# Projections and six gates of the second block moved into one stage of seven-product pairs

## The chip, the cores and the metric

One core of a Trainium2 chip. The metric is the device time of one execution in microseconds (us), median of the runs. All arrays are float32; one launch computes everything.

## The reference, cut to what matters

Two transformer-like blocks run one after the other on 1024 tokens of width 1024. The change touches only the head of the second one:

```python
xn   = rmsnorm_2(x, attn_norm_g)                  # (1024, 1024)
proj = xn @ w_in                                  # pool 512 | dilated q,k,v 3*768 | stick q,k,v 3*512 | s5 512
y_pool, y_dil, y_sb, y_s5 = pool_mixer(...), dilated_attention(...), stick_breaking_attention(...), s5_mixer(...)
for bi, yb in enumerate((y_pool, y_dil, y_sb, y_s5)):
    gate   = sigmoid(xn @ w_gate[bi])             # 4 gates of 1024 x 1024
    merged = merged + gate * (yb @ w_branch[bi])
x = x + merged @ w_out
```

The four gates depend on `xn` alone; the mixers depend on `proj` alone. Here `x` of the second block is the first block's output after `final_norm`.

## The kernel before, in words

The residual stream lies feature-major: eight tiles of 128 features by 1024 tokens. Every matmul keeps float32 accuracy by three products: an operand is split into a high part (`fp32r`) by ScalarE and the rest by VectorE (`split`, L380 to L387), and `gemm` (L351) adds high*high, high*low and low*high. One **tile** of a projection (128 output features, all 1024 tokens) is 8 steps of the contraction x 3 products x 2 halves of 512 tokens, so 48 matmuls. `load_w` (L326) fetches its 512 KB of weights on SyncE's queue (SP) and splits them.

The feed-forward stages already use another form: `pair` (L886) computes two output tiles together with seven products of half size instead of eight (Strassen-Winograd), each product being 4 steps x 3 = 12 matmuls, so 84 for two tiles. It needs the sums T1 to T4 and quarters B11, B21, B22 of the input (`factors`, L845), four sums of weights on POOL and five adds on VectorE. `up` (L957) starts three pairs side by side and then runs one after the other.

Order of the second block before:

- `block2_norm` (L1566) closes the first block's feed-forward: per half of 512 tokens eight output tiles, two sums of squares (VectorE and POOL), the norm, and the split into `xh`, `xl` (16 slots). `early` runs the left half of two stick projections while the right half's norm is due. The residual goes to DRAM (`xd`).
- `stick` (L1640): v by token-major products, then four heads. Each head runs two `chain`s of latency-bound steps; between them `heads` projects the next head's q and k (2 tiles).
- `dilated` (L1750): three groups. Each projects 4 tiles (q, k), from the second on also 2 tiles of v, then runs 8 softmax steps; its bias table goes through DRAM (`ED`, `hk`).
- `s5` (L1953): a preamble of small VectorE operations beside token-major products, then four quarters `q`. In each quarter POOL builds `CL`, `BL`; PE transposes; VectorE copies `U`, builds `Ec` and `Es`, scans, and forms `Y`. `pool` (L2254) projects 4 tiles on the way. Then the `glu` products.
- `merge` (L2305): loads the gates, multiplies branches, in the order 1, 2, 0, 3.

The 32 gate tiles (`gate`, L2287) are computed as **filler**: `fill` (L300) pops the next gate from a list and is called at set places: 1 in `stick`, 15 in `dilated`, up to 19 in `s5`, of which 16 find a gate. A gate is stored to DRAM and read back by `merge`.

Who orders the work: except in the first stage (`manual_schedule`), a planner at compile time orders each engine's instructions. It prefers program order and lets a later instruction go ahead when the earlier one has no data or no buffer in its model. So buffers decide how far it can reach: big tiles share one set of 31 slots (`s4`), PSUM has two 1024-wide buffers and four of 512, and a stage's own pool of SBUF (`fp`) is free for the next stage's pool only when its tiles are released.

Of the kernel before, what the change touches and what calls it, by code (L numbers as in the profile page):

```python
# [18 lines left out]
P = 128  # L19
D = 1024  # L20
# [17 lines left out]
ORDER = (1, 2, 0, 3)  # L38

# [216 lines left out]
class Kern:  # L256
# [193 lines left out]
    def rstd_twice(self, out1, out2, acc, accg):  # L450
# [11 lines left out]
        self.bcast(out2, r2)  # L462
        self.bcast(out1, r1)

# [492 lines left out]
    def up(self, fp, W, B, steps, hidden):  # L957
# [8 lines left out]
        run = lambda j, *first: self.pair(fp, W[j], W[NF + j], B, lambda a: hidden(j, a), gated, *first)  # L966
        p, q = self.pmm(), self.pmm()
        g = [run(0, (p[:, 0:HT], q[:, HT:T])), run(1, (p[:, HT:T], None)), run(2, (q[:, 0:HT], None))]
        for n in range(6):
            if n > 1:  # L970
                next(steps)
            for i in g:
                next(i)
        next(steps)
        for i in g:
            next(i)
# [3 lines left out]
        for j in range(4, NF):  # L980
# [8 lines left out]
        return out  # L989
# [546 lines left out]
    def block1_ffn(self, xd, B, steps):  # L1536
# [15 lines left out]
        with tc.tile_pool(name="f1d", bufs=1) as fp:  # L1552
# [9 lines left out]
            self.block2_norm(xs, out)  # L1562
# [3 lines left out]
    def block2_norm(self, xs, out):  # L1566
        nc, A = self.nc, self.A
        gg = self.gg
        self.xh = [self.big("xh", F32R) for _ in range(KC)]
        self.xl = [self.big("xl", F32R) for _ in range(KC)]  # L1570
        self.xd = [self.dp.tile([P, T], F32, name=self.nm("xd"), tag=f"xd{k}") for k in range(KC)]
        r1, r2 = self.big("r1"), self.big("r2")

        def norm(k, h):
            sl = slice(h * HT, (h + 1) * HT)
            self.norm_split(xs[k][:, sl], r2[:, sl], gg[:, k : k + 1], None, self.xh[k][:, sl], self.xl[k][:, sl], low=nc.gpsimd if h == 0 else nc.vector)

        self.xh2, self.xl2 = self.halves(self.xh), self.halves(self.xl)
        self.first = []
# [8 lines left out]
        for h in range(2):  # L1588
            sl = slice(h * HT, (h + 1) * HT)
            acc = self.big("acc")  # L1590
            for m in range(KC):
                out(m, h)
                self.sumsq(acc[:, 0:HT], xs[m][:, sl], m == 0)
                self.sumsq(acc[:, HT:T], xs[m][:, sl], m == 0, g=self.smc("final_norm", m), eng=nc.gpsimd)
                if h == 1:
                    norm(m, 0)
            if h == 1:
                early(0)
                early(4)
            self.rstd_twice(r1[:, sl], r2[:, sl], acc[:, 0:HT], acc[:, HT:T])  # L1600
        for k in range(KC):
            norm(k, 1)
        for k in range(KC):
            self.dump(f"x2{k}", xs[k])
            nc.vector.scalar_tensor_tensor(xs[k], xs[k], self.smc("final_norm", k), r1, ALU.mult, ALU.mult)
            nc.sync.dma_start(self.xd[k], xs[k])
            self.dump(f"xb{k}", xs[k])
            if self.dbg and "xn0" in self.dbg:
                self.dump(f"xn{k}", self.xh[k].bitcast(F32))


# [28 lines left out]
    def stick(self):  # L1640
# [4 lines left out]
        def heads(h):  # L1645
            r = []
            for m in (h, 4 + h):
                hi, lo = self.big("sqh", F32R), self.big("sql", F32R)
                scale = 128 ** -0.5 if m < 4 else None
                if h:  # L1650
# [772 lines left out]
```

## Time and profile before

| | us |
|---|---|
| median of 3 runs (3452.68 to 3458.37) | 3456.63 |
| the profiled execution | 3452.84 |
| its span, first to last instruction | 3451.0 |
| TensorE busy, 15699 matmuls | 3312.0 |
| VectorE busy | 2092.2 |
| ScalarE busy | 1311.0 |
| POOL busy | 654.7 |

The page gives busy time per engine, the span in slices, the chain that ended last and the costliest groups; the trace behind it can be asked for a window, a tile or an engine's timeline. Matmuls overlap, so their mean duration (about 400 ns for 512 columns) is longer than the distance from one to the next. In a table of windows the number in brackets is the count of instructions; the last three columns are the granted TensorE clock (1 is full speed), the share of the DMA engines and GB/s.

### The profile page before, as it was taken

What the parts mean: (1) busy time and instruction counts of PE and PEld (TensorE: products, weight loads), DVE (VectorE), ACT (ScalarE), POOL (GpSimd) and SP (SyncE); (2) the same over time, 40 slices, a digit from 0 to 9 for tenths busy, and PEclk for the clock granted to TensorE, in tenths of its full rate; (3) what the DMA queues carried; (4) which work ended last, traced back from release to release, by engine and by line L of the source; (5) the groups of instructions that cost most, each with busy time, mean ns of one, the idle gap of its engine ahead of it and who ended that gap; (6) DMA issues with size and microseconds to landing.
All of it is one profiled execution on the core that took longest, in us unless ns stands there. A gap on an engine that the chain in (4) does not pass through costs nothing. (4 is left out here: it accounts for less than half of the span.)

```text
span 3451.0 us, 42496 instructions
## 1 busy us (share of the span) xinstructions
PE 3312.0 (96%) x15699; PEld 2635.8 (76%) x15699; DVE 2092.2 (61%) x3955; ACT 1311.0 (38%) x2471; POOL 654.7 (19%) x510
## 2 busy tenths in 40 slices
PE   6999998989999999899999999999999989999998
PEld 4797776768888777777877778787878768888777
DVE  8746787686565797677332237466265764434886
ACT  5224655454444334356242332222222443333332
POOL 3200000152221441200000002221032142321530
PEclk9999999999999999999999999999999999999999
DMA  6545112422221432201121112222464322223232
GB/s 235 199 151 181 42 59 90 143 85 81 80 80 58 168 94 84 98 31 37 51 65 52 63 55 97 72 90 87 163 227 156 132 98 86 79 85 126 89 93 78
DMA packets 139953, 348.60 MB, mean 101 GB/s; under 512 B 16713, under 2 KB 41697, under 8 KB 139745
## 3 DMA queue, kind: packets, MB, share of 16 engines
q1 hardware_dynamic: 139744, 345.88, 29.7%
q8 instruction: 124, 2.03, 0.2%
q14 instruction: 85, 0.69, 0.1%
HBM read 270.67 MB, written 75.16 MB: 100 GB/s over the span
## 5 line engine op out<-in xcount | busy, mean ns | idle before, releaser
L382 ACT ACTIVATE wh<-w 128x512 fp32r<-128x512 f32 (+1 forms) x508 | 308.4, 610 | 1035.2 <-PE mm L360 734.5
L383 DVE TENSOR_TENSOR wl<-w,wh 128x512 fp32r<-128x512 f32 (+1 forms) x508 | 365.3, 723 | 512.6 <-ACT wh L382 491.5
L358 PE MATMUL mm<-bh,wh 128*128 128x512 f32 x1376 | 532.9, 401 | 26.7 <-ACT a L904 6.2
L362 PE MATMUL mm<-bh,wl 128*128 128x512 f32 x1376 | 523.6, 396 | 4.0 <-DVE wl L383 3.8
L360 PE MATMUL mm<-bl,wh 128*128 128x512 f32 x1376 | 526.3, 396 | 0.2 <-DVE bl L383 0.2
L358 PEld LDWEIGHTS mm<-bh,wh 128*128 128x128 f32 x1376 | 259.8, 189 | 110.2 <-DVE x L2364 11.7
L362 PEld LDWEIGHTS mm<-bh,wl 128*128 128x128 f32 x1376 | 259.7, 189 | 68.7 <-DVE wl L383 7.6
L362 PE MATMUL mm<-xh,wl 128*128 128x512 f32 x944 | 311.7, 401 | 0.0
L358 PE MATMUL mm<-xh,wh 128*128 128x512 f32 x944 | 308.9, 403 | 1.9 <-DVE sql L386 1.9
L360 PEld LDWEIGHTS mm<-bl,wh 128*128 128x128 f32 x1376 | 260.0, 189 | 57.8 <-DVE bl L383 0.6
L360 PE MATMUL mm<-xl,wh 128*128 128x512 f32 x944 | 304.1, 399 | 0.0
L896 POOL TENSOR_TENSOR ws<-w 128x512 f32<-128x512 f32 x44 | 67.0, 1523 | 850.3 <-DMA w<-in_w_up_dram 510.0
L362 PEld LDWEIGHTS mm<-xh,wl 128*128 128x128 f32 x944 | 176.8, 188 | 43.9 <-issue 5.8
L360 PEld LDWEIGHTS mm<-xl,wh 128*128 128x128 f32 x944 | 177.8, 189 | 40.8 <-issue 2.0
L358 PEld LDWEIGHTS mm<-xh,wh 128*128 128x128 f32 x944 | 174.3, 188 | 44.8 <-issue 5.1
L382 ACT ACTIVATE wh<-ws 128x512 fp32r<-128x512 f32 x176 | 110.7, 630 | 202.0 <-PE mm L360 171.9
L362 PE MATMUL ax<-bh,wl 128*128 128x512 f32 x416 | 165.3, 397 | 4.2 <-DVE wl L383 4.2
L360 PE MATMUL ax<-bl,wh 128*128 128x512 f32 x416 | 165.9, 399 | 2.2 <-DVE bl L383 2.1
L358 PE MATMUL ax<-bh,wh 128*128 128x512 f32 x416 | 165.8, 398 | 1.6 <-ACT bh L382 1.6
L383 DVE TENSOR_TENSOR wl<-ws,wh 128x512 fp32r<-128x512 f32 x176 | 137.6, 783 | 27.0 <-ACT wh L382 26.8
L1553 DVE SCALAR_TENSOR_TENSOR x<-mm,adaT,x 128x512 f32<-128x512 f32 (+1 forms) x104 | 85.4, 828 | 40.3 <-PE mm L362 40.0
L1932 POOL TENSOR_TENSOR E<-e,seld 32x1024 fp32r<-32x1024 f32 x3 | 8.2, 2733 | 476.8 <-issue 476.2
(639 smaller groups left out, 6849.9 us busy)
## 6 DMA issues: line engine op xcount, KB each, us to landing
w<-in_w_up_dram SPq DMA_DIRECT2D x88, 512.0 KB
wa<-in_w_ada_dram SPq DMA_DIRECT2D x64, 512.0 KB
w<-in_w_out_dram SPq DMA_DIRECT2D x32, 512.0 KB
w<-in_w_gate_dram SPq DMA_DIRECT2D x32, 512.0 KB
gd<-gf SPq DMA_DIRECT2D x32, 512.0 KB
g<-gd SPq DMA_DIRECT2D x32, 512.0 KB
y<-y SPq DMA_DIRECT2D x28, 512.0 KB
w<-in_w_down_dram SPq DMA_DIRECT2D x24, 512.0 KB
```

The costliest lines, as they stand in the source:

```text
L358: nc.tensor.matmul(ps, lhsT=wh, rhs=xh[k], start=s, stop=False, **kw)
L360: nc.tensor.matmul(ps, lhsT=wh, rhs=xl[k], start=False, stop=False, **kw)
L362: nc.tensor.matmul(ps, lhsT=wl, rhs=xh[k], start=False, stop=e, **kw)
L382: first = nc.scalar.activation(hi, src, AF.Copy)
L383: nc.vector.tensor_tensor(lo, src, hi.bitcast(F32), ALU.subtract)
L896: nc.gpsimd.tensor_tensor(t, x, y, op)
L1553: add = lambda m, x, ps: nc.vector.scalar_tensor_tensor(x, ps, self.adaT[:, 40 + m : 41 + m], x, ALU.mult, ALU.add)
L1932: eng.tensor_tensor(E.rearrange("p (n t) -> p n t", n=8), e.bitcast(F32).unsqueeze(1).to_broadcast([32, 8, P]), seld[:, 256:264].unsqueeze ...
```

## The change

`block2_norm` now also builds the factors of the pair form, storing the residual to DRAM before the norm (`xr`). A new stage `project2` computes 17 pairs: 8 stick tiles, 4 pool, 12 dilated q and k, 4 dilated v, and 6 of the 32 gates. Results go to DRAM, already scaled and in the dilated order. The mixers load them. `xd` is computed in that stage from `xr`. T1 lies for a time in the place of a quarter of `xh`, which is stored as `b12` and restored at the end. The filler is called six times more in `stick` (7 in all), as before in `dilated` (15), so 4 gates are left for `s5`. The diff, cut:

```diff
+GATES = ((3, 0), (3, 1), (3, 2), (3, 3), (3, 4), (3, 5))
     def block2_norm(self, xs, out):
-        def early(m):
-            hi, lo = self.load_w(A["w_sbqk"][m], D)
-            ps = self.pax()
-            self.gemm(hi, lo, [(ps, self.xh2[0], self.xl2[0])])
-            self.first.append((ps, hi, lo))
...
+        B = {"B11": parts(0, lo4), "T1": parts(1, lo4), "B21": parts(0, hi4), "B22": parts(1, hi4)}
...
+                nc.sync.dma_start(self.xr[m][:, sl], xs[m][:, sl])
                 if h == 1:
-                    norm(m, 0)
-            if h == 1:
-                early(0)
-                early(4)
+                    norm(m, L)
+                    self.split(xs[m][:, L], self.xh2[0][m], self.xl2[0][m])
+            row = self.rstd_twice(self.r1[:, sl], r2[:, sl], acc[:, 0:HT], acc[:, HT:T])
+        return B, self.factors2(xs, B, norm, row)
...
+    def project2(self, fp, B, steps):
...
+        jobs = [(sq(h), sq(4 + h)) for h in range(4)] + [(po(0), po(1)), (po(2), po(3))] + [(dq(2 * i), dq(2 * i + 1)) for i in range(6)] + [(dv(0), dv(1)), (dv(2), dv(3))]
+        jobs += [(ga(*GATES[i]), ga(*GATES[i + 1])) for i in range(0, len(GATES), 2)]
+        def run(j, *first):
+            def store(i, h, src):
+                _, d, scale, s, f = jobs[j][i]
+                if i == 0 and s == 1 and scale == 1.0 and f == AF.Copy:
+                    nc.sync.dma_start(d[:, h * HT : (h + 1) * HT], src)
+                    return
+                t = self.sm.tile([P, HT], F32, tag=("it", "dt")[h], name=self.nm("pj"), bufs=2)
+                nc.scalar.activation(t.rearrange("p (s l) -> p l s", s=s), src.rearrange("p (l s) -> p l s", s=s), f, scale=scale)
+                n = HT // s
+                nc.sync.dma_start(d.rearrange("p (s l) -> p s l", s=s)[:, :, h * n : (h + 1) * n], t.rearrange("p (s l) -> p s l", s=s))
...
+            return self.pair(fp, jobs[j][0][0], jobs[j][1][0], B, first_row, out, *first)
+        def residual():
...
+                nc.sync.dma_start(x, self.xr[k])
+                nc.vector.scalar_tensor_tensor(x, x, self.smc("final_norm", k), self.r1, ALU.mult, ALU.mult)
+                nc.sync.dma_start(self.xd[k], x)
+        self.rows(run, len(jobs), steps, residual)
+        for k in range(4):
...
+            nc.sync.dma_start(t, self.b12[k])
+            self.split(t, self.xh2[1][k], self.xl2[1][k])
     def stick(self):
-                    wh, wl = self.load_w(A["w_sbqk"][m], D)
-                    ps = self.pmm(1)
-                    self.gemm(wh, wl, self.xtargets(ps, self.xh2, self.xl2))
-                    last = self.split(ps, hi, lo, scale=scale)
+                nc.sync.dma_start(t, self.sqd[m])
+                last = self.split(t, hi, lo)
...
                 if h < 3:
-                    qk, _ = heads(h + 1)
-                else:
-                    self.fill(None, turn=1, raw=True)
+                    qk, _ = heads(h + 1, fp)
+                self.fill(fp, turn=1, raw=True)
                 for _ in run[1]:
                     pass
+                if h < 3:
+                    self.fill(fp, turn=1, raw=True)
     def dilated(self):
-                        hi, lo = self.load_w(A["w_dvf"][2 * (g - 1) + m], D)
-                        self.gemm(hi, lo, self.xtargets(ps, self.xh2, self.xl2))
+                        nc.sync.dma_start(t, self.dvd[2 * (g - 1) + m])
-                    hi, lo = self.load_w(A["w_dqk"][4 * g + m], D)
-                    self.gemm(hi, lo, self.xtargets(ps, self.xh2, self.xl2))
+                    nc.sync.dma_start(t, self.dqd[4 * g + m])
-                nt = [self.big("num") for _ in range(2)]
+                nt = [fp.tile([P, T], F32, name=self.nm("num")), self.big("num")]
     def pool(self, fp, out):
-            hi, lo = self.load_w(A["w_pool"][g], D)
-            self.gemm(hi, lo, self.xtargets(ps, self.xh2, self.xl2))
+            nc.sync.dma_start(u, self.ud[g])
```

`up`'s loop over pairs is moved unchanged into `rows`, which `up` and `project2` both call. `factors2` has `factors`' five steps, on the halves named above. A gate computed in `project2` is taken off the filler's list and stored after its tanh.

## Rows read from the trace of the kernel before

**Rows 1.** The page, part 1: busy time of TensorE and its share of the span.

```profile
PE 3312.0 (96%) x15699; PEld 2635.8 (76%) x15699; DVE 2092.2 (61%) x3955; ACT 1311.0 (38%) x2471; POOL 654.7 (19%) x510
```

**Rows 2.** Stage windows: busy us (instructions) of PE, PEld, DVE, ACT, POOL; clock; DMA share, GB/s.

```profile
1380.00:1411.00 31.00, 21.62 (x93) 16.15 (x92) 28.69 (x38) 14.81 (x23) 18.84 (x11) 0.89 0.30 102
...
1460.00:1658.00 198.00, 195.49 (x859) 143.33 (x858) 143.50 (x324) 107.21 (x226) 4.79 (x8) 1.00 0.09 30
1658.00:2112.00 454.00, 451.87 (x2355) 347.58 (x2354) 136.54 (x379) 143.57 (x342) 8.20 (x3) 0.99 0.20 62
...
2240.00:2300.00 60.00, 59.14 (x298) 47.57 (x297) 37.70 (x115) 15.19 (x24) 15.10 (x18) 1.00 0.28 89
...
2112.00:2434.00 322.00, 318.42 (x1541) 265.20 (x1541) 196.12 (x616) 85.22 (x153) 65.71 (x81) 1.00 0.27 90
```

**Rows 3.** Timeline of ACT in dilated: evacuations of two neighbouring projection tiles (start, us).

```profile
1817.00 2.02 ACT L1807 ACTIVATE dvf<-mm 128x1024 f32<-128x1024 f32 x1
...
1828.13 2.02 ACT L1807 ACTIVATE dvf<-mm 128x1024 f32<-128x1024 f32 x1
```

**Rows 4.** Stage windows: steady up stage, and the starts of the two up stages.

```profile
840.00:860.00 20.00, 20.00 (x88) 16.18 (x87) 12.05 (x16) 8.09 (x12) 5.70 (x5) 1.00 0.22 79
660.00:760.00 100.00, 87.22 (x343) 67.19 (x342) 86.24 (x105) 50.08 (x80) 51.38 (x32) 0.91 0.18 62
2740.00:2820.00 80.00, 69.76 (x286) 53.57 (x286) 65.18 (x90) 35.36 (x59) 35.13 (x23) 0.96 0.23 76
```

**Rows 5.** Tiles gf, u and y5h: ACT's reads of gates and pool tiles; first glu matmul.

```profile
L2291 ACT ACTIVATE gf<-mm x32: 1003/1007/1027, 1630.6 to 2456.9; 128x1024 f32<-128x1024 f32 x32
...
L2265 ACT ACTIVATE u<-mm x4: 1005/1006/1011, 2193.8 to 2377.6; 128x1024 f32<-128x1024 f32 x4
...
L358 PEld LDWEIGHTS mm<-y5h,wh x64: 187/188/192, 2434.1 to 2488.8; 128*128 128x128 f32 x64
```

**Rows 6.** Timeline of DVE: first U copy; second quarter's first, one weight split, last.

```profile
2190.57 0.69 DVE L2147 COPY U<-ax 128x512 f32<-128x512 f32 x1 [3.23 <-PE ax L2141]
...
2252.74 0.69 DVE L2147 COPY U<-ax 128x512 f32<-128x512 f32 x1 [3.87 <-DMA TP<-KD]
...
2255.77 0.68 DVE L383 TENSOR_TENSOR wl<-w,wh 128x512 fp32r<-128x512 f32 x1
...
2289.43 0.69 DVE L2214 TENSOR_TENSOR Y<-ax,Y 128x512 f32<-128x512 f32 x1 [1.09 <-PE ax L2212]
```

**Rows 7.** Timeline of POOL in S5: one quarter's first and last operation.

```profile
2228.34 2.15 POOL L2110 TENSOR_TENSOR CL<-C,Lrs 128x1152 f32<-128x1152 f32 x1 [63.75 <-PE ax L2212]
...
2242.43 2.39 POOL L2134 TENSOR_TENSOR BL<-BL,BT 128x1024 f32<-128x1024 f32 x1
```

**Rows 8.** Timeline of PE, second quarter: start and end of its first product group.

```profile
2255.05 0.38 PE L2183 MATMUL ax<-U,RT 128*128 128x128 f32 x2
...
2258.40 0.39 PE L2183 MATMUL ax<-U,RS 128*128 128x128 f32 x2
```

**Rows 9.** Timeline of DVE in dilated: softmax steps, then the next group's bias.

```profile
1748.32 0.43 DVE L1853 CUSTOM_DVE_ANT_0 ds<-ax,bias 128x256 f32<-128x256 f32 x1
...
1755.75 0.42 DVE L1853 CUSTOM_DVE_ANT_0 ds<-ax,bias 128x256 f32<-128x256 f32 x1 [0.77 <-PE ax L1850]
...
1793.66 0.17 DVE L1856 TENSOR_SCALAR nm<-mst 128x4 f32<-128x4 f32 x1
...
1803.02 0.54 DVE L1773 TENSOR_TENSOR ng<-ax,ng 4x384 f32<-4x384 f32 x1
...
1815.57 0.86 DVE L1783 COPY bias<-ax 128x256 f32<-128x256 f32 x2 [3.10 <-PE ax L1781]
```

**Rows 10.** Timeline of SP at the border of stick and dilated.

```profile
1655.73 0.34 SPq L1756 DMA_DIRECT2D tab<-in_rel_bias_dram  x1
...
1658.48 0.34 SPq L1636 DMA_DIRECT2D ysb<-osb  x1
```

**Rows 11.** Tile bh: splits of the branch inputs of the merge.

```profile
L382 ACT ACTIVATE bh<-yb x10: 1046/1058/1066, 2463.7 to 2553.2; 128x1024 fp32r<-128x1024 f32 x10
```

More of the change, by code (lines that the diff above doesn't have):

```diff
@@ L966, in up, with rows @@
         run = lambda j, *first: self.pair(fp, W[j], W[NF + j], B, lambda a: hidden(j, a), gated, *first)
+        self.rows(run, NF, steps)
+        return out
+    def rows(self, run, n, steps, each=lambda: None):
         p, q = self.pmm(), self.pmm()
         g = [run(0, (p[:, 0:HT], q[:, HT:T])), run(1, (p[:, HT:T], None)), run(2, (q[:, 0:HT], None))]
-        for n in range(6):
-            if n > 1:
+        for i in range(6):
+            if i > 1:
                 next(steps)
-            for i in g:
-                next(i)
+            for r in g:
+                next(r)
         next(steps)
-        for i in g:
-            next(i)
+        for r in g:
+            next(r)
         cur = run(3)
@@ L979, in up @@
             next(cur)
-        for j in range(4, NF):
+        for j in range(4, n):
+            each()
             new = run(j)
@@ L1594, in block2_norm @@
                 self.sumsq(acc[:, HT:T], xs[m][:, sl], m == 0, g=self.smc("final_norm", m), eng=nc.gpsimd)
+                self.dump(f"x2{m}", xs[m])
+                nc.sync.dma_start(self.xr[m][:, sl], xs[m][:, sl])
                 if h == 1:
-                    norm(m, 0)
-            if h == 1:
-                early(0)
-                early(4)
[L1600 to L1609, printed above, removed]
+                    norm(m, L)
+                    self.split(xs[m][:, L], self.xh2[0][m], self.xl2[0][m])
@@ new lines, in block2_norm, with factors2, split @@
+            row = self.rstd_twice(self.r1[:, sl], r2[:, sl], acc[:, 0:HT], acc[:, HT:T])
+        return B, self.factors2(xs, B, norm, row)
+    def factors2(self, xs, B, norm, row):
+        nc = self.nc
+        L, R = slice(0, HT), slice(HT, T)
+        sub = lambda eng, o, x, y: eng.tensor_tensor(o, x, y, ALU.subtract)
+        pairs = list(zip(xs[:4], xs[4:]))
+        def split(name, k, t):
+            if name not in B or len(B[name][0]) <= k:
+                pair = [self.half_tiles(2, n) for n in ("bh", "bl")]
+                for i in range(2):
+                    B.setdefault(name, ([], []))[i].extend(pair[i])
+            hi, lo = B[name]
+            self.split(t, hi[k], lo[k])
+        for k, (x, y) in enumerate(pairs):
+            norm(k, R, row)
+            nc.sync.dma_start(self.b12[k], x[:, R])
+            t = self.sm.tile([P, HT], F32, tag="it", name=self.nm("t1"), bufs=2)
+            sub(nc.vector, t, x[:, R], x[:, L])
+            split("T1", k, t)
+        yield
+        for k, (x, y) in enumerate(pairs):
+            norm(k + 4, R)
+            sub(nc.gpsimd, x[:, R], y[:, R], x[:, R])
+            split("B22", k, y[:, R])
+        yield
+        for k, (x, y) in enumerate(pairs):
+            nc.vector.tensor_tensor(x[:, L], x[:, R], x[:, L], ALU.add)
+            split("T2", k, x[:, L])
+        yield
+        for k, (x, y) in enumerate(pairs):
+            sub(nc.gpsimd, y[:, L], y[:, L], x[:, L])
+            split("T3", k, x[:, R])
+        yield
+        for k, (x, y) in enumerate(pairs):
+            split("T4", k, y[:, L])
+        yield
@@ L1643, in stick, with heads @@
         vs = []
[L1645 removed]
+        def heads(h, fp):
             r = []
             for m in (h, 4 + h):
[L1648 to L1660 removed]
+                t, hi, lo = fp.tile([P, T], F32, tag="sq", name=self.nm("sq"), bufs=2), self.big("sqh", F32R), self.big("sql", F32R)
+                nc.sync.dma_start(t, self.sqd[m])
+                last = self.split(t, hi, lo)
                 r += [hi, lo]
@@ L1665, in stick @@
             wh, wl = self.tm_weights(A["w_sbv"], 512, vp)
-            qk, last = heads(0)
+            qk, last = heads(0, vp)
             with tc.issue_after(last.ins):
```

68 lines of the change are left out of this document (40 added, 28 removed).

## The prediction

> **What bounds the kernel now.** I read the busy times first: TensorE (PE) is busy for 96% of the span [rows 1]. Then the windows by stage, because a mean hides where the cover comes from: in stick and in dilated PE idles 2.5 of 198 us and 2.1 of 454 us, and in S5, up to the first glu product, 3.6 of 322 us [rows 2]. So from 1411 us on a matmul removed is time gained, as long as something else is there to run. But look at the other columns of the S5 window: VectorE is busy for 196 of the 322 us, far more than the 137 of 454 in dilated. The mixers are chains of short steps; PE is full only because projections and gates are poured between them. The reader should see two things: PE is the bound, and in S5 VectorE is a close second, kept off the path by filler alone. Times below go against the profiled execution, 3452.84 us, of which 1.8 lie outside the span; the median shown is 3456.63, 3.8 more, and I add that at the end. About 0.2% (7 us) is what a measurement of this kernel can tell from no change.
>
> **What the stage of pairs saves.** A projection tile of 48 matmuls takes 11.13 us when such tiles follow each other [rows 3]. 34 tiles move: 8 + 4 + 12 + 4 + 6, or 34 x 11.13 = 378.4 us. In a steady up stage 88 matmuls take 20 us [rows 4], so a pair of 84 takes 19.09, and 17 pairs 324.5. Gain: 53.9 us. Of this 204 matmuls (2448 less 17 x 12 = 204) explain 46; the rest is that products with one target run at 0.227 us each, those with two at 0.232. The engines beside PE carry a pair as in the up stage, where VectorE is busy 12, ScalarE 8 and POOL 6 of 20 us [rows 4]; the scaled stores add four ScalarE copies a pair (a strided one of 1024 columns took 2.0 us [rows 3], so up to 4 us). All of it lies beside PE: nothing to pay.
>
> **DMAs.** The change issues per pair four half stores, for the mixers 28 loads, and for the residual and b12 some 32 more: roughly 128 issues at 0.34 us of SP's time [rows 10], 44 us of that queue spread over 700. A store waits on ScalarE and holds up the weight loads behind it on SP; these have three buffers, as in the up stages, which also store a tile per pair without a gap. I cost this at nothing; if the cover fails, a pair would lose an issue or two, under 1 us, 17 us in all.
>
> **The start of the stage.** Before, between 1380 and 1411, 93 matmuls run where 31 us at full pace hold 136 [rows 2]: 43 x 0.227 = 9.8 us lost. The pair form starts as the up stages do. These lose 97 x 0.227 = 22 us (343 of 440 matmuls) and 66 x 0.227 = 15 us (286 of 352) [rows 4]. The second is nearer, since its norm has no bias step, as here. Cost 15 - 9.8 = +5, bounds 0 and +12; I take +6, as the sums of squares are doubled here. The end of the stage, where the v weights of stick wait for room and a split: nothing shows it; between 0 and 5, I take +2.
>
> **Stick.** Before it covers its chains with 6 tiles of heads and 1 gate, after with 7 gates: the same 7 x 11.13 us of work, none of it awaited by the next head any more. 0, bounds -3 and +3. Seven gates need a tanh in the merge: 7 x 1.0 us [rows 5] of ScalarE, hidden by the products there.
>
> **Dilated.** 16 projection tiles (178 us) go; 15 gates stay. A softmax step without interference takes 7.43 us from one to the next [rows 9], so two need 14.9, while PE has a gate (11.1) and the products of two steps to do for them, which fills it. That part stays bound by PE. What was covered is the change of group: the last softmax step ends its VectorE part at 1793.7, the bias chain starts at 1803.0 and ends 13.4 us later, at 1816.4 [rows 9], while six projection tiles run. Now there is one gate (11.1 us) the planner can pull into that gap, and then it is missing later. Twice over: 0 at best, 2 x 14 = 28 at worst. I take +8, nearer to the low end, since the two loops have 24 steps x 7.43 = 178 us for 15 x 11.1 = 167 us of gates plus their own products, so PE is still nearly full.
>
> **S5, the term that decides.** `fill` finds 32 gates before; after, 6 + 7 + 15 are gone, so 4 are left where S5 had 16. With the 4 pool tiles, 15 tiles (15 x 11.13 = 167 us) vanish ahead of the first glu product (of the 12 gates that go, one stood inside glu: the last gate is read at 2456.9, the first glu product loads at 2434.1 [rows 5]). The four left are used up in the preamble and the first quarter. Quarters two to four then have no filler at all. What does such a quarter take? Its VectorE part runs from the first U to the last Y, 2252.7 to 2290.1, or 37.4 us; five weight splits of 0.68 go with the filler (3.4), and 2 us were waits on PE: 32 us remain [rows 6]. PE's own work in a quarter is what is left of the 62.2 us between two first U copies after four tiles of filler, about 18 us. So PE would idle at least 14 us in each. Is 32 reachable? Only if the planner lets the next quarter's Ec, Es and BL run ahead. Before, it could not: xh and xl held 16 of the 31 slots to the last gate. After, they are free from the first quarter on, so mostly yes. I take 35 a quarter. Then: the first U at about 2180 instead of 2190.6 (the pool tile ahead of it is gone), the first quarter 34.6 (two gates' splits), three of 35, and 8 us to the first glu product (an estimate: a gelu, a copy and a split of 1024 columns, at the 1.0 us of u's reads and the 1.06 of yb's splits [rows 5, 11], transposes, and a wait behind each): 2180 + 34.6 + 105 + 8 = 2327.6. It comes 106.5 us earlier, where 167 us of PE's work went: **60 us of new idle time**. Ends: VectorE never idle after 2112 gives 196 - 30 x 0.68 = 175.7 us against PE's 318.4 - 167 = 151.4 [rows 2], 24 us of idle; no overlap between quarters gives 51.5 a quarter (below), 110 us.
>
> **Sum.** -53.9 + 6 + 2 + 0 + 8 + 60 = +22 us: 3452.8 + 22 = 3475 for a profiled execution, 3478.7 against the median; I say 3478. The saving is real, and S5 hands it back: the projections were worth more as cover than as work.
>
> **A rule on the clock.** In the 31 us around the norm, where PE has gaps, the mean granted clock was 0.89, against 1.00 in the steady up stage [rows 2, 4]; so part of that stretch ran at the lower of its two levels (1.2 instead of 2.4 GHz), after PE had idled. In the bare quarters PE would be busy about half the time. A quarter's first product group of 32 takes 3.6 us [rows 8]; the second has as many, and the transposes and swaps together about as many columns again, some 11.6 us (an estimate). At half the clock that is +11.6 a quarter if VectorE has nothing else to do meanwhile, 35 us in all, so 3513; if it has, nothing, and I take nothing. The Trainium skill ("TensorE: Matmul & The Clock Gate", section "Why this matters for your kernels") says that gaps between bursts of matmuls throw the engine back to half its rate and so speaks against this change; the trace agrees that the clock falls, and no run here shows it in S5.
>
> **Rivals.**
> 1. *S5 refilled: faster.* The merge's products of branches 1 and 2 need only dilated's and stick's outputs: 12 and 24 matmuls for each of 8 tiles, 2 x 144 x 0.232 = 67 us. If the planner pulled them into the bare quarters, or if VectorE ran without a gap from the preamble on (24 us of idle), the S5 term falls to 24 or less: -53.9 + 16 + 24 = -14, about 3443; with the merge's products fully drawn ahead 3420. The point from which it decides: S5's new idle under 38 us. For it: 16 slots come free. Against: a stage's own buffers seem to wait for the stage before; dilated's first table is only fetched at 1655.7, three us before stick's last store [rows 10], and the merge's tiles are such buffers; before, the branch inputs are split from 2463.7 on, behind glu's start [rows 11]. Chance 0.2.
> 2. *Serial quarters: much slower.* The slots are freed, but the planner does not use them: POOL needs 16.5 us from CL to the last BL [rows 7], then 1 to 2 us of transposes, then VectorE's 34: 51.5 us a quarter, 16.5 more than I take, so +50, or 3528. Before, the 64 us that POOL sat idle before CL, until PE's last product, show that CL has only one buffer [rows 7], which speaks for it; that CT is built a quarter ahead speaks against. Chance 0.1.
> 3. *The clock*: PE at the lower level through the bare quarters and on the path, 3513. Chance 0.1.
> 4. *A tie*: the ends of all terms lean the right way, S5 40 to 48, dilated 0 to 4: 3450 to 3463. Chance 0.18.
> The forecast itself, 3464 to 3500, has 0.42.
>
> **How the numbers follow.** Slower: 0.42 + 0.1 + 0.1 = 0.62; same 0.18; faster 0.2. The range leaves out the far half of rival 1 and most of rival 2: 3438 to 3515.
>
> **What would show it.** Right: a stretch of some 320 us of pairs at 88 matmuls per 20 us; dilated about 165 to 175 us shorter; in S5 three quarters of 32 to 38 us with PE busy half of each and VectorE almost always; total PE idle up by 65 to 90. Wrong: quarters under 28 us or PE busy through S5 (then a net gain of 14 or more), or PE gaps inside the stage of pairs, which would mean that SP or ScalarE paces it.

## The result, and the profile after

The changed kernel takes 3571.3 us (median of 4 runs, 3569.0 to 3573.0) against 3457.5 for the kernel before: ratio 1.0328, 95% interval 1.0313 to 1.0344. That is 114 us slower, where 22 were forecast; the sign was right, the size far outside the range. The profiled execution has a span of 3569.2 us, 118.2 more than before.

The page of the changed kernel, part 1 (busy us, share of the span, instructions), to be held against [rows 1]:

```profile
PE 3309.3 (93%) x15495; PEld 2625.9 (74%) x15495; DVE 2181.4 (61%) x4081; ACT 1405.8 (39%) x2635; POOL 744.1 (21%) x578
```

The 204 matmuls are gone, as the change says. But PE idles 259.9 us where it idled 139.0, and its busy time fell by 2.7 us only, though 204 matmuls at the 0.23 us of [rows 4] are some 46: more of it now lies at a lower granted clock, 0.66 to 0.88 in windows below. To see where, I cut both spans at the same events: dilated's first copy of v (`vd`), S5's first copy of a token product (`X`), the first `U`, the first glu product (`y5h`). Tiles of the changed kernel (line, count, duration in ns, first and last start):

```profile
L1885 ACT ACTIVATE vd<-ax x8: 385/385/387, 2005.8 to 2025.7; 128x256 f32<-128x256 f32 x8
...
L2042 ACT ACTIVATE X<-ax x32: 271/281/298, 2287.2 to 2329.1; 128x128 f32<-128x128 f32 x32
...
L2223 DVE COPY U<-ax x8: 681/691/692, 2357.4 to 2516.6; 128x512 f32<-128x512 f32 x8
...
L360 PE MATMUL mm<-y5h,wh x64: 389/394/792, 2557.7 to 2604.0; 128*128 128x512 f32 x64
```

The same of the kernel before (U and glu are in [rows 5, 6]):

```profile
L1799 ACT ACTIVATE vd<-ax x8: 384/384/384, 1675.6 to 1695.5; 128x256 f32<-128x256 f32 x8
...
L1966 ACT ACTIVATE X<-ax x32: 272/282/301, 2119.3 to 2157.1; 128x128 f32<-128x128 f32 x32
```

Both are cut at 1384, where the first block's last product has started in the kernel before; in the changed kernel 12 of its products, 3 us, come behind that. The column "forecast" holds the prediction's terms, laid on the same stretches (the first row is 17 pairs, 324.5, less eight tiles, plus six gates, plus 8 for start and end; the last is the one gate inside glu):

| stretch | before | after | change | forecast | off by |
|---|---|---|---|---|---|
| 1384 to first `vd` | 291.6 | 621.8 | +330.2 | +310.3 | +20 |
| to first `X` (dilated) | 443.7 | 281.4 | -162.3 | -170.1 | +8 |
| to first `U` (preamble) | 71.3 | 70.2 | -1.1 | -10.6 | +10 |
| to first glu product (quarters) | 243.5 | 200.3 | -43.2 | -95.9 | +53 |
| to the end | 1016.9 | 1011.5 | -5.4 | -11.1 | +6 |

More than half of the miss is in the four quarters. One boundary of theirs in the changed kernel, first VectorE, then POOL, then PE (start, us; in brackets the idle time before it and what ended it):

```profile
2393.44 0.69 DVE L2290 TENSOR_TENSOR Y<-ax,Y 128x512 f32<-128x512 f32 x1 [0.87 <-PE ax L2288]
2410.95 0.69 DVE L2223 COPY U<-ax 128x512 f32<-128x512 f32 x1 [16.82 <-PE ax L2217]
...
2411.70 0.17 DVE L2236 TENSOR_TENSOR Ec<-Ec,ph 128x8 f32<-128x8 f32 x1
...
2463.28 0.69 DVE L2223 COPY U<-ax 128x512 f32<-128x512 f32 x1 [16.87 <-PE ax L2217]
```

```profile
2393.48 2.14 POOL L2186 TENSOR_TENSOR CL<-C,Lrs 128x1152 f32<-128x1152 f32 x1 [57.95 <-PE ax L2288]
2395.70 2.63 POOL L2188 TENSOR_TENSOR CL<-CL,CT 128x1152 f32<-128x1152 f32 x1
2398.42 2.14 POOL L2187 TENSOR_TENSOR CT<-C,Lin 128x1152 f32<-128x1152 f32 x1
2400.51 0.41 POOL L2208 TENSOR_TENSOR BL<-Bb,Lr 128x128 f32<-128x128 f32 x1
...
2406.55 2.34 POOL L2210 TENSOR_TENSOR BL<-BL,BT 128x1024 f32<-128x1024 f32 x1
```

```profile
2408.94 0.48 PE L2216 MATMUL ax<-const,BL 128*128 128x128 f32 x1 [6.96 <-POOL BL L2210]
...
2436.41 3.75 PE L2271 MATMUL ax<-S,swp 128*128 128x512 f32 x4 [20.02 <-DVE S L2265]
```

Read them in a circle. The quarter's last product frees `CL`, POOL starts it at once (2393.48), builds `BL` behind it, PE transposes `BL`, and only then VectorE gets `U`, 16.82 us after its last step; PE then waits 20.02 us for VectorE. Nothing of the next quarter runs ahead: a quarter from U to U is 52.3 us (2410.95 to 2463.28). Windows of the changed kernel (columns as in [rows 2]): the start of the stage of pairs, its steady part without and with the last pair's end, three quarters:

```profile
1384.00:1470.00 86.00, 68.61 (x268) 52.78 (x269) 74.41 (x100) 37.74 (x66) 39.15 (x27) 0.88 0.32 109
...
1470.00:1750.00 280.00, 278.69 (x1198) 224.46 (x1197) 105.23 (x146) 126.84 (x195) 71.21 (x53) 1.00 0.40 131
1470.00:1751.70 281.70, 280.38 (x1205) 225.81 (x1204) 106.10 (x147) 128.54 (x197) 71.21 (x53) 1.00 0.40 132
...
2357.00:2410.00 53.00, 35.66 (x175) 26.72 (x174) 32.41 (x108) 12.83 (x19) 15.17 (x20) 0.80 0.26 83
2410.00:2463.00 53.00, 22.00 (x118) 17.03 (x117) 31.96 (x107) 7.92 (x13) 15.16 (x20) 0.69 0.15 46
2463.00:2515.00 52.00, 22.31 (x115) 16.75 (x115) 33.14 (x110) 8.20 (x14) 13.03 (x19) 0.66 0.11 33
```

VectorE's 32 and POOL's 15 us of a quarter add up to 47 of its 53. The start of the stage holds 236 products (268 less 32 small ones of the norm) where 86 us hold 371 at 0.2315 us each, the pace of a steady up stage in a window of 200 us (shown further down). The steady part runs almost without a gap.

### The profile page after: what moved, and what is told of

Read it like the earlier page. It is cut to its first block, busy times and chain, and to the rows that moved or that the text cites. A ratio compares the mean times of both kernels' runs of the same rounds, so it can differ in the third digit from the quotient of the medians.

```text
span 3569.2 us, 42917 instructions
## 1 busy us (share of the span) xinstructions
PE 3309.3 (93%) x15495; PEld 2625.9 (74%) x15495; DVE 2181.4 (61%) x4081; ACT 1405.8 (39%) x2635; POOL 744.1 (21%) x578
## 4 chain that ended last, share of the span: by engine, by line
PE 48%; DVE 5%; POOL 2%; issue 1%; DMA 1%; ACT 1%; SPq 0%; DVEq 0%; POOLq 0%; ACTq 0%
PE mm L360 11%; PE mm L362 11%; PE mm L364 11%; PE ax L362 2%; PE ax L360 2%; PE ax L364 2%; PE ax L1782 1%; PE ax L1726 1%; PE ax L1725 1%; PE ax L1727 1%; PE mm L1782 1%; DVE bl L385 1%; DMA hk<-ED 1%; PE ax L1926 1%; PE ax L1939 1%
## 5 line engine op out<-in xcount | busy, mean ns | idle before, releaser
L360 PE MATMUL mm<-bh,wh 128*128 128x512 f32 x1580 | 614.7, 401 | 31.7 <-ACT a L907 9.0
L364 PE MATMUL mm<-bh,wl 128*128 128x512 f32 x1580 | 606.1, 398 | 5.0 <-DVE wl L385 4.9
L362 PE MATMUL mm<-bl,wh 128*128 128x512 f32 x1580 | 609.0, 397 | 0.4 <-DVE bl L385 0.4
L360 PE MATMUL mm<-xh,wh 128*128 128x512 f32 x544 | 195.2, 411 | 2.4 <-DVE x L1561 1.8
L364 PE MATMUL mm<-xh,wl 128*128 128x512 f32 x544 | 196.6, 412 | 0.0
L362 PE MATMUL mm<-xl,wh 128*128 128x512 f32 x544 | 196.4, 412 | 0.0
L899 POOL TENSOR_TENSOR ws<-ws,w 128x512 f32<-128x512 f32 x61 | 82.2, 1348 | 210.0 <-DMA w<-in_w_up_dram 153.8
L364 PEld LDWEIGHTS mm<-xh,wl 128*128 128x128 f32 x544 | 102.8, 192 | 29.3 <-issue 8.9
L360 PEld LDWEIGHTS mm<-xh,wh 128*128 128x128 f32 x544 | 103.6, 193 | 28.1 <-issue 3.4
L362 PEld LDWEIGHTS mm<-xl,wh 128*128 128x128 f32 x544 | 103.5, 193 | 27.2 <-issue 6.6
```

What stands on the lines that cost most here:

```text
L360: nc.tensor.matmul(ps, lhsT=wh, rhs=xh[k], start=s, stop=False, **kw)
L362: nc.tensor.matmul(ps, lhsT=wh, rhs=xl[k], start=False, stop=False, **kw)
L364: nc.tensor.matmul(ps, lhsT=wl, rhs=xh[k], start=False, stop=e, **kw)
L899: nc.gpsimd.tensor_tensor(t, x, y, op)
```

## The experiments

All were timed against the kernel before in the same session (3453 to 3460); times are medians. The changed kernel's 3571.3 comes from a session of its own, so a gain against it is uncertain by some 5 us, and one of 8 or 10 us by half its size.

**Each stage's loss by itself.** Three kernels: one takes S5's cover away from the kernel before, one dilated's, and one keeps S5 and stick as they were beside a stage of eight pairs.

*S5 stripped, kernel before (3405.8).*

```diff
     def fill(self, fp, bufs=1, turn=None, raw=False):
         if self.todo:
             b, m = self.todo.pop(0)
+            if len(self.todo) < 12:
+                self.gd[b, m] = self.gd[0, 1]
+                return
...
-            hi, lo = self.load_w(A["w_pool"][g], D)
...
-            nc.scalar.activation(u, ps, AF.Copy)
+            nc.sync.dma_start(u, self.xd[g])
```

> The kernel before with its S5 stripped as the change strips it: the last 12 gates of the list are not computed (the merge reads another gate's tile in their place), and pool's four projections are left out (their tiles are loaded from the residual in memory). 16 tiles, 178 us of PE's work, are missing; everything else is the kernel before. It measures S5's cover by itself, without the stage of pairs. Prediction on record (60 us of new idle): 3457 - 178 + 60 = 3339. Theory S with the lengths of the changed kernel's trace (S5 from its first token product's copy to the first glu product 270.5 us instead of 314.8, the rest 5.4 less): 3457 - 50 = 3407, and up to 10 more if PE's clock also falls at the change from dilated to S5.

Ratio 0.9861 (0.9843 to 0.9878): 50.5 us gained for 178.1 us of work, so 127.6 us of cover lost (124 to 136 by the interval), not 60. No pair is in this kernel, and its quarters are those of the changed kernel:

```profile
L2150 DVE COPY U<-ax x8: 681/692/692, 2196.3 to 2355.6; 128x512 f32<-128x512 f32 x8
...
L361 PE MATMUL mm<-y5h,wh x64: 387/396/793, 2396.7 to 2443.0; 128*128 128x512 f32 x64
```

From the first U to the first glu product 200.4 us, against 200.3 in the changed kernel. S5's loss has nothing to do with how the projections are computed elsewhere.

*Dilated stripped, kernel before (3289.1):* q, k and the later groups' v are loaded (`nc.sync.dma_start(t, self.xd[...])`) in place of their 16 projections.

> The kernel before with dilated's 16 projections left out (q, k and the two later groups' v are loaded from the residual in memory instead), all 15 gates and everything else as before. 178 us of PE's work are missing; what the time falls short of that is dilated's loss of cover by itself. Prediction on record: 8 us, 0 to 28: 3456 - 178 + 8 = 3286. By the changed kernel's trace (from dilated's first v copy to S5's first X copy 281.4 us, before 443.7): 16 us, 3294.

Ratio 0.9517 (0.9502 to 0.9532), so 167 us gained for 178: 11 us of cover lost, 6 to 16 by the interval. The forecast of 8 stands. Part of it lies where it was forecast: PE's waits for the bias tables are 5.9 us in seven pieces, where there were 1.3 in three.

*Pairs for dilated's 16 tiles alone, all cover as before (3476.0):* `jobs` holds six pairs `dq` and two `dv`; stick's heads, pool and `fill` as in the kernel before.

> The stage of pairs with dilated's 16 tiles alone (8 pairs); stick's heads, pool and all 32 gates as in the kernel before, so S5 and stick have the cover that they had. Theory R (the rest of the loss is the stage itself): 8 pairs save 8 x 2.8 = 22 us, the start costs 15 more than before (236 products between 1384 and 1470 where 86 us hold 371), the end of the stage 4, dilated without its projections 16: 3456 + 13 = 3469, 3462 to 3476. Rival Q (the stage is sound and only S5 loses): 3456 - 22 + 6 = 3440.

Ratio 1.0055 (1.0035 to 1.0075), 12 to 26 us slower, as theory R said; rival Q's 3440 failed. Its profiled execution is the fastest of the four (3464.8), so what follows divides 12 us and not the 18 of the medians. In it S5 takes what it took before (first `X` to first glu product 314.7 us, before 314.8), dilated loses 13.3, and the stretch ahead of dilated grows by 176.7, of which eight pairs are 155.6: 21 us for the start and the end of the stage.

**Why the quarters are serial.** Four orders of the same work, each on the changed kernel.

*Two buffers for `CL` (3561.0):* `bufs=2` in its line.

> The changed kernel with one line different: CL, the tile that POOL builds at the head of each S5 quarter, has two buffers instead of one. Theory S (POOL's queue): in the changed kernel a quarter lasts 52.3 us because POOL starts CL only at the previous quarter's last product (2393.48, 2445.77, 2499.69), and BL is queued behind it; BL's transposes hold up U, and VectorE sits idle 16.8 us before each U. With a second buffer CL and BL are built ahead, and quarters two to four take some 36 us: 3 x 16 = 48 us less, 3523. Rival V (VectorE and a PE at the lower clock set the quarter anyway): U moves earlier, but the wait turns up behind it; under 10 us gained, 3562 to 3571. Rival D (POOL's work now runs beside VectorE's and slows it): about 30 us gained, 3540.

10 us gained, where theory S said 48: S failed as it stood. POOL used the second buffer to build a `CL` ahead and then stood, 52.41 us, at the `CL` after that, with the next `BL` still behind it. So the second quarter's `U` waits 16.82 us as before, the third's 14.65, and only the fourth's, with no further `CL` ahead of its `BL`, 5.21. POOL, then VectorE:

```profile
2402.62 2.15 POOL L2186 TENSOR_TENSOR CL<-C,Lrs 128x1152 f32<-128x1152 f32 x1 [52.41 <-PE ax L2288]
```

```profile
2420.09 0.69 DVE L2223 COPY U<-ax 128x512 f32<-128x512 f32 x1 [16.82 <-PE ax L2217]
...
2515.70 0.69 DVE L2223 COPY U<-ax 128x512 f32<-128x512 f32 x1 [5.21 <-PE ax L2217]
```

A buffer where the wait shows helps little here, since the queue behind it keeps its order.

*`BL` ahead of `CL`, in buffers of its own (3563.8):*

```diff
+                BL = fp.tile([P, T], F32, tag="BL", name=self.nm("BL")).rearrange(...)
+                BT = fp.tile([P, T], F32, tag="BT", name=self.nm("BT")).rearrange(...)
...
                 CL = fp.tile([P, 8, 9, 16], F32, tag="CL", name=self.nm("CL"))
```

> The changed kernel; BL and BT get two buffers of their own in S5's pool instead of slots, and BL is written ahead of CL in the program, so that POOL builds BL of the next quarter before it comes to the CL that waits. Two buffers for CL alone brought only 10 us: POOL then took the CL of the quarter after next before the next BL, and its wait moved on (52.41 us before CL, U again 16.8 us late). Theory S (POOL's order holds up U): now U follows Y at once, quarters two to four take 36 us instead of 52.3, and the time is 3571 - 3 x 16 = 3523. Rival V (something else behind it, PE's transposes at the lower clock or a slot for U): 3555 or more.

8 us, not 48: S failed in its simple form. `BL` is now built a quarter ahead, but `U` still comes 9.31 us late, since its transposes stand on PE behind the products of `CL` and `Bb`, and VectorE got slower.

*The transposes and `U` ahead of `CL` as well (3538.8):* the block from `RT, RS` to the copy of `U` moves up too.

> The changed kernel with BL in buffers of its own and, in the program, BL, its transposes and U ahead of CL and of CL's products with Bb. With BL alone ahead, U still came 9.3 us late (PE's transposes stood behind the products that wait for CL), and VectorE's steps for Ec and Es ran beside POOL's BL and took longer (one of 128x16 took 2.31 us instead of 0.17; U to S 29 us instead of 24). Theory S2 (an order of queues, and a price for POOL beside VectorE): the transposes now wait only for the gelu of the quarter before, U comes some 4 us after Y, the stretching by 5 us stays: a quarter of 44 instead of 52.3, 3571 - 3 x 8 = 3547. If there were no such price: 39, 3531. Rival V (no order helps): 3560.

33 us, more than S2's 24; quarters of 46 (first copies of U at 2393.41, 2439.69 and 2485.44), and the first `U` comes 9 us earlier.

*Only `Ec` and `Es` ahead of `CL` (3550.7):*

```diff
             for q in range(4):
...
+                Ec, Es = v8(self.big("Ec")), v8(self.big("Es"))
+                ...
                 CL = fp.tile([P, 8, 9, 16], F32, tag="CL", name=self.nm("CL"))
```

> The changed kernel; only the block that builds Ec and Es is written at the head of a quarter, ahead of CL, instead of behind U. POOL's and PE's orders stay. VectorE then has the 10 to 13 us of that block to do in the 16.8 us in which it waits for U. Theory S2 (the quarter is serial because VectorE's order puts work that needs nothing behind the one that waits): a quarter is CL and BL on POOL, 15.4 us, stretched to some 18 beside VectorE, then transposes, rho's products and 16 us to the last Y: 38 to 41 instead of 52.3; 3571 - 3 x 12.5 = 3533. Rival V (a shared port makes POOL and VectorE serial whatever the order): 3555 to 3571.

21 us, quarters of 46: between S2's 38 us (3533) and rival V (3555), and nearer to V. VectorE no longer waits for `U` at all, yet little more than a third of the 16.8 us was won. Its timeline (steps over 0.6 us) and POOL's at the same place show why:

```profile
2437.79 0.69 DVE L2291 TENSOR_TENSOR Y<-ax,Y 128x512 f32<-128x512 f32 x1 [0.87 <-PE ax L2289]
...
2438.54 1.47 DVE L2193 TENSOR_TENSOR Ec<-Ec,ph 128x8 f32<-128x8 f32 x1
...
2440.12 2.60 DVE L2195 TENSOR_TENSOR Ec<-Ec,tb 128x8 f32<-128x8 f32 x1
...
2442.96 2.00 DVE L2198 TENSOR_TENSOR Es<-Es,tb 128x8 f32<-128x8 f32 x1
```

```profile
2437.84 2.15 POOL L2211 TENSOR_TENSOR CL<-C,Lrs 128x1152 f32<-128x1152 f32 x1 [30.57 <-PE ax L2289]
2440.06 2.63 POOL L2213 TENSOR_TENSOR CL<-CL,CT 128x1152 f32<-128x1152 f32 x1
2442.77 2.16 POOL L2212 TENSOR_TENSOR CT<-C,Lin 128x1152 f32<-128x1152 f32 x1
```

A step of 128x8, 0.17 us when POOL is idle (2411.70 above), ends here each time within 0.04 us after the POOL operation beside it. So the two engines take turns, and VectorE's busy time in a stretch of 46 us is 42, not 32 (two quarters):

```profile
2408.00:2454.00 46.00, 23.98 (x113) 18.47 (x112) 42.10 (x106) 7.94 (x13) 15.46 (x20) 0.69 0.15 48
2454.00:2500.00 46.00, 24.83 (x117) 19.07 (x116) 41.87 (x111) 7.94 (x13) 13.30 (x19) 0.72 0.12 41
```

10 of POOL's 15 us come on top of VectorE's 32. Both orders that brought `U` forward stop at 46 us; whether another does better, and what S5 would take with POOL's work elsewhere, was not tried.

**Does the clock matter?** Products that nobody reads keep PE running in the quarters (8 + 8 in the first run, 20 + 14 in the second).

```diff
+                pd = self.pmm(0)
+                for i in range(20):
+                    nc.tensor.matmul(pd[:, 0:HT], lhsT=swp, rhs=U[:, 0:4].rearrange("p g c -> p (g c)"), start=True, stop=True)
                 V.tensor_tensor(rho, rho, rt, ALU.add)
```

> The changed kernel with products in S5's quarters whose result nobody reads: eight behind the rho products (they need U) and eight behind Y's (they need H), each 128x512 like the swap. They do not wait for VectorE in the stretch that they fill and should lift the granted clock (0.66 to 0.80 in the quarters). Theory K (PE's lower clock is on the quarters' path): the swap, 3.75 us, and the transposes at twice the pace, 52.3 becomes 47 to 49, and the time is 3550 to 3558. Rival (VectorE and POOL set the length alone): 3568 to 3575; if the products get in the way, more.

> The changed kernel with more of the products that nobody reads: 20 behind the rho products (0.88 us each, so 17.6 of the 20 us before the swap) and 14 behind Y's. With eight and eight the mean granted clock rose from 0.67 to 0.80 and the quarters stayed 53.1 us, but PE had idled 12 us before the swap, which still took 3.75 us, so it did not tell. Now the swap should take 2.2 us, the transposes 1.7 instead of 3.4. Theory K (the lower clock is on the path): 3 to 5 us a quarter less, 3552 to 3560. Rival: PE's pace is hidden by VectorE's and POOL's: 3568 to 3575. If the added products delay CL's products: 3580.

3574.6 and 3582.6: theory K's times failed in both. The first did not tell, since PE still idled ahead of the swap. The second did lift the mean clock; a window of it, two product groups of PE, and VectorE's U in two neighbouring quarters:

```profile
2415.00:2470.00 55.00, 49.65 (x207) 29.00 (x206) 34.55 (x123) 9.75 (x19) 15.18 (x20) 0.97 0.15 44
```

```profile
2440.54 3.44 PE L2274 MATMUL ax<-S,swp 128*128 128x512 f32 x4 [3.48 <-DVE S L2268]
...
2463.35 1.92 PE L2194 MATMUL ax<-CL,Bb 128*16 128x128 f32 x16
```

```profile
2415.18 0.69 DVE L2223 COPY U<-ax 128x512 f32<-128x512 f32 x1 [15.95 <-PE ax L2217]
...
2467.27 0.69 DVE L2223 COPY U<-ax 128x512 f32<-128x512 f32 x1 [16.02 <-PE ax L2217]
```

The products of `CL` and `Bb` take 1.92 us (3.46 in the changed kernel), the clock is 0.97, and the quarter is 52.1 instead of 52.3 us. Only the swap, ahead of which PE still idles 3.48 us, stayed slow (3.44 us, where 2.2 were expected), so some 1.2 us a quarter remain untested. Apart from that the lower clock costs the quarters nothing that can be measured. The 11 us more come from the first quarter (62.1 us from U to U instead of 53.5) and from the way from the last U to glu (51 us instead of 41), where 14 added products stand ahead of the last transposes; elsewhere some 8 us are won back, which was not traced.

**The start of the stage.** `factors2` has eight subtractions on POOL; this run puts them on VectorE, the engine that was thought to be full (3561.3).

```diff
-            sub(nc.gpsimd, x[:, R], y[:, R], x[:, R])
+            sub(nc.vector, x[:, R], y[:, R], x[:, R])
```

> The changed kernel with the eight subtractions of the stage's factors on VectorE instead of POOL. Theory L (an operation with two operands in memory on POOL holds up VectorE's for as long as it lasts): the eight take POOL 13.6 us, beside which VectorE's splits take 1.36 us instead of 0.68; on VectorE they take 8 x 0.68 = 5.4. The start gets 4 to 8 us shorter: 3564 to 3567. Rival (VectorE is simply full): 5.4 us more on the engine that paces the start, 3576.

10 us gained by the medians, though one execution of four took 3572.8; the forecast was 4 to 8, the rival's 3576 failed. In the changed kernel three splits take 4.09 us beside three subtractions of 5.10 (VectorE, then POOL):

```profile
1443.14 4.09 DVE L385 TENSOR_TENSOR bl<-x,bh 128x512 fp32r<-128x512 f32 x3
```

```profile
1440.99 5.10 POOL L1613 TENSOR_TENSOR x<-x,x 128x512 f32<-128x512 f32 x3 [1.83 <-DVE x L1637]
```

With the subtractions on VectorE each step takes 0.68 (1.88 for three), and the window of the start holds 22 products more, 5 us:

```profile
1434.58 0.68 DVE L1613 TENSOR_TENSOR x<-x,x 128x512 f32<-128x512 f32 x1
```

```profile
1384.00:1470.00 86.00, 73.28 (x290) 57.39 (x291) 72.23 (x110) 40.13 (x71) 32.09 (x20) 0.88 0.30 108
```

A rival would be that something waited for POOL's slower subtraction itself. But no wait of this window in the changed kernel is put down to a subtraction on POOL, which leaves the shared time.

*The same edit in the up stages of the kernel before, without the change (3444.7).*

> The kernel before, with the subtractions of its up stages' factors (eight in each of two stages) on VectorE instead of POOL; nothing of the change in it. Theory L: in these starts, too, single VectorE operations of 0.68 us last 1.78 beside POOL's; moving the subtractions gives 3 to 8 us a stage, so 3456 becomes 3440 to 3450, faster than both kernels. Rival (VectorE is full there, POOL's share free): 3456 to 3466.

Ratio 0.9954 (0.9941 to 0.9968): faster than both kernels. The first up stage starts with 374 matmuls where [rows 4] has 343:

```profile
660.00:760.00 100.00, 91.01 (x374) 71.37 (x373) 85.60 (x117) 51.88 (x84) 43.61 (x24) 0.95 0.24 81
```

**Do the causes add up?** `GATES = ()` gives six gates back to S5, alone and with the orders above. Each line below the first is `GATES` empty with the one edit named; the last has the edits of the line above it too.

| kernel | us |
|---|---|
| changed, `GATES` empty | 3516.9 |
| and two buffers for `CL` | 3506.9 |
| and `Ec`, `Es` first | 3507.0 |
| and `BL` of its own, first | 3499.6 |
| and transposes and `U` first | 3494.3 |
| and the subtractions of all three stages on VectorE | 3474.4 |

> The changed kernel with no gates in the stage of pairs: its list GATES is empty, 14 pairs instead of 17, and S5 finds 10 gates to pour in instead of 4. Theory C (S5 lacks cover): the six gates fit into the idle time that PE has in the quarters (some 30 us of 52 in each), so the stage gets 3 x 19.5 = 58 us shorter and S5 not longer: 3513. If the granted clock in the quarters also rises from 0.6 to 0.8 to near 1 and PE's slow pace was on the path, up to 5 us a quarter more come back: 3495 to 3500. Rival N (the quarters' waits can't be filled, since gates wait for the same VectorE and PSUM): S5 gets longer by most of 6 x 11.1 = 67 us, and the time is 3560 to 3580.

> Both edits: GATES empty and two buffers for CL. If S and C both hold: a quarter has 18 us of PE's own work and two gates (22 us), so 40 us where PE binds, against 52 in the changed kernel: 3513 less 3 x 12 = 3477. If the gates fill what the single CL leaves idle anyway (C without S), no more than 5 us under the kernel with GATES empty. Were the two gains to add up in full, 3571 - 58 - 48 = 3465.

> The same order with GATES empty: 14 pairs, ten gates for S5. The gates came in for 4 us in all when the quarter was 53 us long (3571 to 3517). With quarters of 40 us PE has 18 us of its own work and two gates of 11.1: 40, just full. S2: 3533 - 54 + 3 x 3 = 3488. If the gates do not fit in the shorter quarter: 3505 or more. A loss of some 30 us against the kernel before would be left: the start of the stage 15, dilated 16, the change to S5 9, and quarters, less the 39 that 14 pairs save.

> The same, with GATES empty (ten gates for S5 instead of four, 14 pairs). Alone the empty list gave 54 us, six gates hidden in idle time at a price of 4. If S holds, a quarter has 18 us of PE's own work and two gates of 11.1, so some 40 us, against 54 with one CL and the gates: 3517 - 3 x 13 = 3478. If the gates and the wait were the same idle time counted twice: 3505 to 3515.

> BL in its own buffers with its transposes and U ahead of CL (alone: 3539, quarters of 44 us), and GATES empty (alone: 3517). PE needs 18 us for its own work in a quarter and 22 for two gates, 40 of 44, so the gates should fit as they did in 53 us: 3539 - 54 + 4 = 3489. If quarters with gates are held up by the gates' weight splits on VectorE (two gates, ten splits of 0.68 a quarter, 7 us): quarters of 48, 3500.

> The changed kernel with U and its transposes ahead of CL, BL in its own buffers, GATES empty, and the subtractions of all three stages' factors on VectorE. If the causes add up: 3494 - 10 (start of the stage of pairs) - 2 x 5 (up stages) = 3474. What is then left against the kernel before with the same subtractions moved is some 28 us: quarters, dilated's cover and the rest of the start, less the 39 that 14 pairs save.

Six gates moved into S5 give 54 of the 58 us that their pairs took: cover is almost free there, as C said. With the gates in place the orders gain 10 (two `CL`), 10 (`Ec` first), 17 (`BL`) and 23 us (`U` first), where they gained 10, 21, 8 and 33 without. So the two orders that had shortened the quarters most lose some of it: the quarters are 56 to 59 us with `Ec` first and 49 to 51 with `U` first, where both were 46. The forecasts of 3477 to 3488 for the first three orders, quarters of 40 with two gates each, failed; 3494 lies between the two named for the fourth. The last line was forecast to the microsecond, with some luck: it counts 10 us for the two up stages, which by themselves gave 15. It is 1.0038 of the kernel before (1.0026 to 1.0051), and 30 us above the best kernel, the one before with its subtractions moved.

## Why the prediction was right in sign and wrong in size

- **The saving.** 17 pairs, "-53.9": mis-sized. I took the pace from "88 matmuls take 20 us", a window so short that one matmul at its edge is a per cent. A window of 200 us of the same stage, kernel before, gives 0.2315 us each; 17 pairs take 330.6 and save 47.8, 6 us less.

```profile
800.00:1000.00 200.00, 200.00 (x864) 161.96 (x863) 118.67 (x145) 82.08 (x122) 54.95 (x43) 1.00 0.23 82
```

- **DMAs, 0: right.** In the steady part PE is busy for 278.7 of 280 us. **Stick, 0: right:** from the last copy of v to dilated 207.7 us, before 208.1.
- **Start and end of the stage, "+6" and "+2", bounds 0 to 12 and 0 to 5: wrong, outside the bounds.** The stretch ahead of dilated grew by 22 us more than its work (330.2 less 330.6 of pairs, plus 22.2 net of tiles taken out and gates put in); the run with eight pairs gave 21. Of it the start is 15 by the count of products: 31 us lost in 86, where the 27 us of the norm before lost 16 (80 products, 31 of them small ones of the norm). Of the rest 3 are the first block's 12 products behind 1384, and 3 more are lost in the stage's later part, 1205 products in 281.7 us. The step that failed was to price the start by the nearest one. The counts were misread besides: the 93, 343 and 286 products of the rows hold 31, 16 and 16 small ones. Without them the three windows lose 17, 26 and 19 us, the cost comes out at +2, and the miss is larger. POOL's share does not set this start apart (39 of 86 us, 35 of 80 in the nearest); its subtractions are worth 5 us of products here. What else makes it longer was not tried.

```profile
1384.00:1411.00 27.00, 18.31 (x80) 13.69 (x79) 24.69 (x34) 12.37 (x19) 15.83 (x10) 0.87 0.30 103
```

- **Dilated, "+8", 0 to 28: right,** 11 by itself, 16 in the changed kernel.
- **S5, "60 us of new idle time", bounds 24 to 110: the step that failed.** 127.6 by itself. The sentence was "After, they are free from the first quarter on, so mostly yes": I let empty slots decide whether the next quarter's steps run ahead. They did not: `BL` stood behind a `CL` that waits for the quarter's last product, `Ec` behind a `U` that waits for `BL`. And the 32 us of VectorE came from a quarter in which POOL's work lay in VectorE's pauses (kernel before, the 16.6 us of [rows 7]: VectorE busy for 3.5, POOL for 16.2); without such pauses most of POOL's time adds. Ahead of the quarters another 10 us are missing: I took the first pool tile to stand before the first U, though the rows have it read at 2193.8 and U at 2190.57 [rows 5, 6].

```profile
2228.30:2244.90 16.60, 16.60 (x84) 13.39 (x83) 3.49 (x3) 6.06 (x8) 16.24 (x20) 1.00 0.30 96
```

- **Rivals.** Rival 2, serial quarters of 51.5 us, is what happened (52.3), and the row that spoke for it, POOL idle until PE's last product [rows 7], was the right one to follow; 0.1 was too little, and its 3528 was short by the terms above. Rival 3, the clock: the clock fell (0.66 to 0.69) and cost the quarters nothing that could be measured. The Trainium skill's rule that gaps between bursts throw the engine back to half its rate ("TensorE: Matmul & The Clock Gate", "Why this matters for your kernels") is borne out by the clock column, but here PE waits for VectorE, and raising the clock to 0.97 left the quarter at 52.1 us.

Of the signs named beforehand, the stage of pairs ran at 86 matmuls per 20 us (88 said), dilated got 162 us shorter (165 to 175 said), PE's idle time rose by 121 (65 to 90), and VectorE, far from always busy in the bare quarters, was busy for 32 of each 52 us.

Measured terms: -47.8 + 22 + 16 + 128 = 118, the difference of the two spans.

What stays open: why the start of this stage loses more than those of the up stages, and what the 6 us between glu and the end are made of.

## What to carry to other kernels

Before filler work is taken out of a stage, ask what that stage would take bare, and read it from its chain: which queue holds an instruction that waits, and what behind it needs nothing. Two engines that are each half busy are no sign of room, if the rows show their operations stretching beside each other; then much of the one's time adds to the other's. A buffer, an order and an engine's share were three separate repairs here, and each alone brought less than the waits it was aimed at.

## What the runs showed of the hardware

**POOL and VectorE take turns.** A VectorE step of 128x8 with two operands in SBUF took 2.60 us beside a POOL addition of 2.63, 0.17 without, and ended 0.03 us after it. The Trainium skill ("GPSIMD Engine Reference", section "1. Specifications") has POOL's SBUF interfaces shared with VectorE, in contention where VectorE reads two SBUF inputs. The traces agree; the runs add the size: up to the whole of the POOL operation, and taking eight subtractions off POOL was worth 10 us in the stage of pairs, sixteen 15 us in the two up stages.

**The clock can fall while PE is busy.** In the kernel before, at the change from dilated to S5, products over 32 partitions follow directly on a gate. PE's timeline and windows there:

```profile
2098.12 8.34 PE L1943 MATMUL ax<-E,selr 32*128 32x512 f32 x22
```

```profile
2098.00:2100.00 2.00, 2.00 (x9) 1.39 (x8) 2.00 (x2) 1.02 (x1) 0.53 (x1) 1.00 0.00 0
...
2102.00:2104.00 2.00, 2.00 (x6) 1.51 (x5) 2.00 (x3) 0.13 (x1) 0.00 (x0) 0.50 1.03 366
...
2108.00:2110.00 2.00, 2.00 (x5) 1.66 (x6) 2.00 (x3) 0.00 (x0) 0.00 (x0) 0.50 0.29 85
...
2112.00:2116.00 4.00, 4.00 (x18) 4.00 (x18) 3.43 (x10) 0.00 (x0) 0.00 (x0) 1.00 0.87 260
```

PE shows hardly any idle time, and the granted clock goes from 1.00 to 0.50 and comes back once products over 128 partitions follow. In the changed kernel such products alternate with a gate's, and the windows there have the low clock for longer:

```profile
2265.00:2275.00 10.00, 10.00 (x19) 4.74 (x18) 4.31 (x6) 1.06 (x1) 0.00 (x0) 0.50 0.17 67
2275.00:2280.00 5.00, 5.00 (x12) 3.13 (x12) 2.78 (x4) 0.00 (x0) 0.00 (x0) 0.50 0.00 0
```

Which of the two kinds of product the clock answers to was not tried by itself.
